# One loop for every group of four heads, a last load in halves, and six held stores in an attention-times-value kernel on Trainium2

**Chip, cores, metric.** One core of one Trainium2 chip. The metric is the device time of one execution in microseconds (us), lower is better; the profile's span is some 2 us shorter, as it runs from the first to the last instruction. Line numbers such as L124 are those of the kernel whose profile is shown; the same loop has another number in each kernel (L134 before is L124 after, L176 is L166, L161 is L151).

## The reference

```python
batch, n_heads, seq, head_dim = 8, 12, 1024, 64          # float32
attn_weights: (8, 12, 1024, 1024)      v: (8, 12, 1024, 64)
return np.einsum('bhqs,bhsd->bhqd', attn_weights, v)     # float32
```

403 MB of weights, 25 MB of v and 25 MB of output pass through the core: 96 heads, 24 groups of four.

## The kernel before

The core works in 48 units. Two units are a group of four heads: 128 partitions are 4 heads by 32, and a partition holds 32 rows of one head, 16 (the `G` row groups) in each unit. GpSimd loads a unit (8.39 MB of fp32, cast to bf16 on the way) into one of two buffers. TensorE transposes its 16 row groups, two bf16 side by side in an fp32 word, through four PSUM banks; VectorE and ScalarE copy them to SBUF; TensorE multiplies by v, the product is copied, transposed back and copied into an output slot. A group is stored as one transfer of 1 MiB. The stores of the last groups are *held*: issued only behind the last load, so that the DMA engines have work while TensorE finishes.

```python
LOOPED = NV - 1                      # 23 groups of four heads in the loop
HELD = 4
HELD_FROM = LOOPED - HELD            # groups 19 to 22 are held
BY_SYNC = HELD_FROM + 2              # 19, 20 by GpSimd; 21, 22 by SyncE
pieces_of = {                        # the last four heads: two units of two heads
    NU - 2: [(0, GH), (GH, GH)],
    NU - 1: [(0, 4), (4, 4), (8, 4), (12, 2), (14, 2)],
}
# ... cut ...
def pe_unit(i, n, loaded, it):       # TensorE, one unit
    pe.wait_ge(*loaded)
    for g in range(G):
        transpose_g(abf[i], g, n)
    wait_both(s_ot, n)
    if i == 0:
        pe.wait_ge(s_vr, it)
        spread_v(range(VH), po + px)
        wait_both(s_vbf, it * 2)
    transpose_back()                 # the unit before
    wait_both(s_last, n)
    # ... cut: 64 matmuls of 256 columns ...
with nc.Fori(1, LOOPED + 1, 1, engines=(PE,)) as it:
    # ... cut: two pe_units ...
for t in range(2):                   # the separate end: a pair of heads each, piece by piece
    # ... cut ...
# GpSimd
for n in range(NU - 2):
    pool.wait_ge(s_t[True], (n + 1) * PER_DVE)   # unit n has left its buffer
    load_attn(n + 2)
    if n % 2 == 0:
        # ... cut: load of v for the next group ...
        if 0 < q <= HELD_FROM:
            store(q - 1)
for q in range(HELD_FROM, BY_SYNC):
    store(q)
pool.drain()
# SyncE
nc.sync.wait_ge(*s_piece[NU - 1, len(pieces_of[NU - 1]) - 1])   # the last load has landed
for q in range(BY_SYNC, LOOPED):
    store(q, by_sync=True)
# ... cut: the last four heads, 0.5 + 0.25 + 0.25 MiB ...
```

## Time and profile before

| | before |
|---|---|
| time, median (range) | 1055.54 us (1055.07 to 1056.22), 4 runs; 1055.86 was the median of the first three, which the prediction knew |
| span | 1053.7 us |
| busy: TensorE, VectorE, ScalarE | 71%, 37%, 38% |
| DMA engines | full from the first to the last but one of 40 slices |
| traffic at HBM | 427.82 MB read, 25.17 MB written: 430 GB/s |

Read it from the bottom up: if the DMA engines are full, the time is the bytes over the rate, plus what isn't full at the start and the end.

### The profile page before, as it was taken

To read this page: it belongs to the slowest core of one execution; us is meant where nothing else is said; L and a number is where in the kernel's file an instruction comes from. 1 tells how busy PE (TensorE), PEld (TensorE's weight loads), DVE (VectorE), ACT (ScalarE), POOL (GpSimd) and SP (SyncE) were. 2 spreads that over 40 slices of the span, in tenths; PEclk is the share of its full clock that TensorE was granted. 3 is DMA by queue.
4 is the path that set the end of the run, shared out by engine and by line. 5 is a ranking of instruction groups with operands and counts; after the bars stand their busy time and mean duration, and the time that the engine had idled before them with its cause. 6 is when DMAs were issued, how large, how long until landed. Compare 5 with 4: busy or idle time off the path is not lost.

```text
span 1053.7 us, 16145 instructions
## 1 busy us (share of the span) xinstructions
PE 753.2 (71%) x6888; PEld 704.7 (67%) x6888; DVE 387.5 (37%) x583; ACT 404.9 (38%) x492; POOL 54.6 (5%) x106
## 2 busy tenths in 40 slices
PE   0877687866877668676786767876767767687796
PEld 0766586755867667675686666866667767677685
DVE  1543334423433234332353333433334333343353
ACT  0443334433443334433353333434334333343353
POOL 1000000000000000000000000000000000000010
PEclk9988878988888888888888878889788888898899
DMA  9999999999999999999999999999999999999998
GB/s 219 220 217 208 238 231 219 239 210 248 235 214 238 207 241 239 218 239 211 244 233 218 233 223 232 238 219 239 229 220 238 213 236 238 219 219 208 218 215 281
DMA packets 15096, 239.70 MB, mean 227 GB/s; under 512 B 1648, under 2 KB 2160, under 8 KB 5488
## 3 DMA queue, kind: packets, MB, share of 16 engines
q0 software_dynamic: 13968, 235.41, 99.6%
q1 hardware_dynamic: 1120, 4.19, 1.0%
q8 instruction: 4, 0.07, 0.0%
q14 instruction: 4, 0.03, 0.0%
HBM read 427.82 MB, written 25.17 MB: 430 GB/s over the span
## 4 chain that ended last, share of the span: by engine, by line
DMA 73%; PE 25%; issue 1%; ACT 0%; DVE 0%; POOL 0%; POOLq 0%; SPq 0%
DMA abf<-in_attn_weights_dram 73%; PE bank L134 23%; PE bank L176 1%; PE bank L161 0%; ACT at L287 0%; PE bank L149 0%; DVE at L287 0%; POOL abf L373 0%; ACT ot L306 0%; ACT osb_last L268 0%; POOLq L476 0%; SPq L83 0%
## 5 line engine op out<-in xcount | busy, mean ns | idle before, releaser
L134 PE MATMUL bank<-ident,abf 128*128 128x128 f32 x3072 | 467.6, 325 | 261.0 <-DMA abf<-in_attn_weights_dram 261.0
L134 PEld LDWEIGHTS bank<-ident,abf 128*128 128x128 f32 x3072 | 458.0, 215 | 274.1 <-DMA abf<-in_attn_weights_dram 273.3
L287 DVE COPY at<-bank 128x1024 bf16<-128x1024 bf16 x480 | 320.0, 688 | 494.0 <-PE bank L134 493.3
L287 ACT COPY at<-bank 128x1024 bf16<-128x1024 bf16 x288 | 289.0, 1012 | 425.4 <-PE bank L134 425.4
L176 PE MATMUL bank<-at,vbf 128*64 128x256 bf16 x3040 | 215.9, 279 | 1.5 <-ACT at L287 1.2
L176 PEld LDWEIGHTS bank<-at,vbf 128*64 128x64 bf16 x3040 | 195.3, 108 | 17.0 <-issue 5.2
L299 ACT COPY ot<-bank 128x512 f32<-128x512 f32 x46 | 26.9, 585 | 173.5 <-PE bank L176 173.5
L299 DVE COPY ot<-bank 128x512 f32<-128x512 f32 x46 | 31.8, 691 | 145.1 <-PE bank L176 145.1
L161 PE MATMUL bank<-ident,ot 128*128 128x128 f32 x392 | 52.4, 276 | 31.4 <-DVE vbf L261 30.9
L373 POOL DMA_DIRECT2D abf<-in_attn_weights_dram x53 | 28.2, 534 | 896.2 <-PE bank L134 895.2
L161 PEld LDWEIGHTS bank<-ident,ot 128*128 128x128 f32 x392 | 43.4, 141 | 43.9 <-DVE vbf L261 42.2
L268 ACT COPY osb<-bank 128x512 f32<-128x512 f32 x94 | 50.5, 589 | 20.8 <-PE bank L161 20.8
L261 DVE CAST vbf<-bank 128x512 bf16<-128x512 f32 x48 | 31.0, 686 | 7.3 <-PE bank L149 7.3
L261 ACT CAST vbf<-bank 128x512 bf16<-128x512 f32 x48 | 25.9, 588 | 11.8 <-PE bank L149 11.8
L149 PE MATMUL bank<-vr,spread 32*128 32x512 bf16 x384 | 26.7, 377 | 0.0
L149 PEld LDWEIGHTS bank<-vr,spread 32*128 32x128 bf16 x384 | 10.2, 92 | 7.3
L385 POOL DMA_DIRECT2D out_dram<-osb x21 | 11.3, 540 | 41.7 <-ACT osb L268 41.7
L378 POOL DMA_DIRECT2D vr<-in_v_dram x23 | 12.1, 528 | 19.2 <-PE bank L149 18.8
L287 ACT ACT_TABLE_LOAD x9 | 11.5, 1283 | 1.2 <-SPq L83 1.1
L306 ACT COPY ot<-bank 128x256 f32<-128x256 f32 (+1 forms) x3 | 1.3, 443 | 9.1 <-PE bank L176 9.1
L306 DVE COPY ot<-bank 128x256 f32<-128x256 f32 (+1 forms) x3 | 1.5, 514 | 7.4 <-PE bank L176 7.4
L360 DVE CAST vr<-v 128x2048 bf16<-128x2048 f32 x1 | 1.3, 1304 | 3.4 <-DMA v<-in_v_dram 3.4
(11 smaller groups left out, 7.1 us busy)
## 6 DMA issues: line engine op xcount, KB each, us to landing
abf<-in_attn_weights_dram POOLq DMA_DIRECT2D x46, 4096.0 KB, 33.3
out_dram<-osb POOLq DMA_DIRECT2D x21, 1024.0 KB, 34.1
vr<-in_v_dram POOLq DMA_DIRECT2D x23, 512.0 KB, 34.4
abf<-in_attn_weights_dram POOLq DMA_DIRECT2D x2, 2048.0 KB, 26.3
abf<-in_attn_weights_dram POOLq DMA_DIRECT2D x3, 1024.0 KB, 20.3
out_dram<-osb SPq DMA_DIRECT2D x2, 1024.0 KB, 8.0
v<-in_v_dram SPq DMA_DIRECT2D x1, 1024.0 KB, 5.0
abf<-in_attn_weights_dram POOLq DMA_DIRECT2D x2, 512.0 KB, 27.6
```

Of the source, the lines that this page charges most:

```text
L134: last = pe.matmul(out=pt[g % 4][:, k], lhsT=words[:, k], rhs=ident, is_transpose=True, start=(k == 0), stop=(k == KW - 1),)
L149: last = pe.matmul(out=ps, lhsT=spread[rows, b], rhs=vr[rows, b], start=(b == 0), stop=(b == VB - 1),)
L161: last = pe.matmul(out=ps[:, ds(j * P, P)], lhsT=ot[:, j0 + j], rhs=ident, is_transpose=True, start=(j == 0), stop=(j == jn - 1),)
L176: last = pe.matmul(out=outs, lhsT=vbf[:, 2 * kw + par, h], rhs=at[:, ds(half * GH + j0, jn), kw, ds(col * np_, np_), par], start=(n == 0), ...
L261: copy(out=vbf[:, :, h], in_=ps.rearrange("p (k d) -> p k d", k=SB)).then_inc(s_vbf[e])
L268: return copy(out=rows.rearrange("p (half j) d -> p j half d", half=2)[:, ds(j0, jn)], in_=ps[:, ds(0, jn * P)].rearrange("p (j half d) -> ...
L287: ins = copy(out=at[:, g].rearrange("c k j two -> c (k j two)"), in_=bank[g % 4].bitcast(bf16),)
L299: copy(out=ot.rearrange("c j (h p) -> c h j p", h=VH)[:, ds(2 * e, 2)], in_=po[e].rearrange("c (h j p) -> c h j p", h=2, j=GH),).then_inc( ...
L306: copy(out=ot.rearrange("c j (h p) -> c h j p", h=2)[:, e, ds(j0, jn)], in_=po[e].rearrange("c (j p) -> c j p", j=GH)[:, ds(j0, jn)],).the ...
L373: pool.dma_start(out=abf[n % 2][:, ds(g0, gn)].rearrange("p g s -> p (g s)"), in_=in_).then_inc(s_abf[n % 2] if k == 0 else s_piece[n, k][ ...
L378: pool.dma_start(out=vr.rearrange("p b x -> p (b x)"), in_=v_g[iv]).then_inc(s_v, 16)
L385: eng.dma_start(out=out_q[q], in_=osb[slot(q)].rearrange("p r d -> p (r d)"), **({} if by_sync else {"single_packet": True}),).then_inc(s_ ...
```

## The change

Its intent: the last four heads are treated as all others, which removes the second code path for pairs of heads. That puts more work behind the last load. Two things are to pay for it: the last two units are loaded in halves, so that only half of the last unit's transposes wait for the last bytes, and six stores are held instead of four. TensorE's loop runs the same code in every turn, so it can't wait for the halves' own semaphores in the last turn alone. SyncE therefore watches all loads in order and tells TensorE of each through one counting semaphore, `s_half`.

```diff
-    HELD = 4
-    HELD_FROM = LOOPED - HELD
-    BY_SYNC = HELD_FROM + 2
+    HELD = 6
+    HELD_FROM = NV - 1 - HELD
+    BY_SYNC = HELD_FROM + 3
 ... cut ...
-    pieces_of = {
-        NU - 2: [(0, GH), (GH, GH)],
-        NU - 1: [(0, 4), (4, 4), (8, 4), (12, 2), (14, 2)],
-    }
+    HALVED = NU - 2
 ... cut ...
             for g in range(G):
+                if g == GH:
+                    pe.wait_ge(s_half, n)
                 transpose_g(abf[i], g, n)
 ... cut ...
-        with nc.Fori(1, LOOPED + 1, 1, engines=(PE,)) as it:
+        with nc.Fori(1, NV + 1, 1, engines=(PE,)) as it:
 ... cut: TensorE's, VectorE's and ScalarE's code for the two pairs, 60 lines, removed ...
         wait_both(s_ot, NU + 1)
-        transpose_back([(0, 4, px[0])])
-        wait_both(s_last, NU)
-        multiply_pair(1, 4, 4)
-        wait_both(s_ot, NU + 2)
-        transpose_back([(4, 2, px[1]), (6, 2, bank[0])])
+        transpose_back()
 ... cut ...
+            pieces = [(0, G)] if n < HALVED else [(0, GH), (GH, GH)]
+            for g0, gn in pieces:
                 pool.dma_start(
 ... cut; the rest is SyncE's ...
+        for n in range(-2, NU - 2):
+
+            if n + 2 < HALVED:
+                nc.sync.wait_ge(s_abf[n % 2], 16 * ((n + 2) // 2 + 1))
+            else:
+                nc.sync.wait_ge(s_second[n + 2], 16)
+            nc.sync.sem_inc(s_half)
 ... cut: v and the stores' slots, as before ...
```

## The prediction

> **What bounds the kernel now.** I began with the page's slices: whichever engine is full in all forty is the bound, and the rest only has to keep it fed.
>
> ```profile
> PE   0877687866877668676786767876767767687796
> DMA  9999999999999999999999999999999999999998
> DMA packets 15096, 239.70 MB, mean 227 GB/s; under 512 B 1648, under 2 KB 2160, under 8 KB 5488
> HBM read 427.82 MB, written 25.17 MB: 430 GB/s over the span
> DMA abf<-in_attn_weights_dram 73%; PE bank L134 23%; PE bank L176 1%; PE bank L161 0%; ACT at L287 0%; PE bank L149 0%; DVE at L287 0%; POOL abf L373 0%; ACT ot L306 0%; ACT osb_last L268 0%; POOLq L476 0%; SPq L83 0%
> ```
>
> The 16 DMA engines are at nine tenths or more from the first slice to the last but one; TensorE is not. The 227 GB/s counts the bf16 that arrives; counted where it is read, as fp32, the traffic is 452.99 MB, 430 GB/s. The chain credits 23% to the transposes (L134), because a buffer is reloaded only when all 16 groups have left it. That is no loss: the other buffer's load is queued meanwhile, so DMA stays full.
>
> Next, the chain of waits in order of time, for what one store costs inside the stream:
>
> ```profile
> 828.90 9.79 PE bank L134 x64
> 872.45 10.15 PE bank L134 x64
> 916.01 10.50 PE bank L134 x64
> 957.11 10.40 PE bank L134 x64
> 998.26 10.35 PE bank L134 x64
> ```
>
> Two units (four heads) take 872.45 - 828.90 = 43.55 us, again 43.56, then 41.10 and 41.15. The short periods are those in which the kernel no longer stores: 2 x 8.389 MB of weights and 1.049 MB of v, 17.83 MB in 41.12 us, 433.5 GB/s. With a 1.049 MB store, 18.87 MB in 43.55 us, 433.4 GB/s. One stored group of four heads therefore costs 43.55 - 41.12 = 2.43 us where it lies, exactly its bytes.
>
> Last, two-microsecond windows over the end (columns: stretch, length, busy time and count of PE, PEld, DVE, ACT, POOL, then PE clock, DMA share, GB/s), and the end in order of time:
>
> ```profile
> 1036.00:1038.00 2.00, 0.84 (x7) 0.65 (x7) 0.82 (x2) 1.89 (x2) 0.00 (x0) 1.00 1.06 287
> 1042.00:1044.00 2.00, 1.65 (x16) 1.39 (x16) 1.25 (x2) 1.50 (x2) 0.00 (x0) 1.00 1.02 426
> 1048.00:1050.00 2.00, 0.00 (x0) 0.00 (x0) 0.00 (x0) 0.00 (x0) 0.00 (x0) 1.00 0.95 353
> 1050.00:1052.00 2.00, 0.00 (x0) 0.00 (x0) 0.00 (x0) 0.00 (x0) 0.00 (x0) 0.90 0.17 58
> ```
> ```profile
> 1039.59 0.82 SPq L385 DMA_DIRECT2D out_dram<-osb  x2
> 1043.76 4.40 SPq L447 DMA_DIRECT2D out_dram<-osb_last  x2
> 1046.56 0.63 PE L161 MATMUL bank<-ident,ot 128*128 128x128 f32 x4 [0.55 <-ACT ot L306]
> 1047.23 0.37 ACT L268 COPY osb_last<-bank 128x256 f32<-128x256 f32 x1 [0.81 <-PE bank L161]
> ```
>
> A store moves as many bytes as it writes, a load twice what it writes, so the GB/s column jumps from some 215 to 425 where loads give way to stores: by mixing the two rates to 287, at about 1037.4. SyncE sees the last load's semaphore at 1039.59, 2.1 us after its data. From 1037.4 the engines are full with stores alone: two held 1 MiB stores of GpSimd, two of SyncE, and the last 1 MiB in three, 5.24 MB; at 425 GB/s 12.3 us, to 1049.7. They drain at about 1050.3 and the span ends 3.4 us later. TensorE's last work is done by 1047.2, the last copy at 1047.6, and the last 0.25 MiB store is issued from 1047.6. So the two ends, drained stores and finished tail, lie within a microsecond of each other.
>
> **What the Trainium skill says.** "DMA: Bandwidth & Descriptors", section "Where 436 GB/s comes from", gives 435.2 GB/s as the fabric's ceiling. The trace agrees: 433.4 GB/s in a steady period, so no rearrangement speeds the stream; only bytes, gaps and the end are left. The same page, "Issuing engines are not separate DMA queues", says that transfers of SyncE and GpSimd share the same 16 engines and interleave; the windows agree, 426 GB/s with both storing, no more than one queue had. Its section "Anatomy of one DMA — SWDGE (gpsimd) path" puts about 2 us of fixed cost mostly on the receipt of the last write; the 2.1 us above and the 3.4 us at the end are of that kind. "TensorE: Matmul & The Clock Gate", "Part 1: The HAM clock gate", says the clock falls to half after about 3.4 us of idleness and returns after as much work. The trace agrees in kind: after 2.73 us of waiting 64 transposes took 8.02 us, after 4.53 us they took 10.35, at a granted 0.50 to 0.54 in the first 4 us.
>
> **The change part by part.** *Bytes.* The last four heads go from two pairs of heads to one group of four. Every weight, v and output byte moves once as before, at the same run lengths in DRAM (1 KB for the last stores). 0 us.
>
> *Held stores.* The loop stored groups 0 to 18; now 0 to 16. Held: 17 to 19 on GpSimd and 20 to 22 on SyncE. Two stores leave the stream of loads, which therefore ends 2 x 2.43 = 4.9 us earlier: data at 1032.5, semaphore at 1034.6. They come back after it: 7.34 MB of stores at 425 GB/s take 17.3 us, to 1049.8, against 1049.7 by the same working before. Sum: about 0. Each store was paid at 2.43 us and is now paid at 2.47.
>
> *The uniform last unit.* Before, the loads of the last unit came in five pieces, and only 2 groups (8 transposes) and half a multiply stood behind the last piece. Now eight groups and the whole multiply do. From the last semaphore, 1034.6: SyncE passes it on, about 0.1 (estimate: the gaps between engines in the chain are 0.02 to 0.28 us); 32 transposes, 4.0 us at the rate of 64 in 8.02 and 5.2 at 64 in 10.35, I take 4.7 as TensorE will have idled about 3 us; unit 46's back transposes 1.04; 64 matmuls 4.48; a gap 0.15; ScalarE's product copy 0.58; a gap 0.15; eight back transposes 1.09; VectorE's copy of the second bank 0.69. Sum 13.0 us, so the last store is issued at 1047.6. By coincidence of design that is where it is issued now, since the loads end 4.9 us earlier and the tail behind them grows from 1047.6 - 1039.6 = 8.0 us to 13.0.
>
> *SyncE's relay.* 48 semaphore increments, and one more wait in each of TensorE's units. The wait stands after eight groups, that is at least 4 us after the unit's load landed in all units but the last two; SyncE passed the same load before. SyncE's other waits in between (v, and a store's receipt, at most 2.4 us longer) lie behind transfers queued ahead of the next load, which needs some 19.4 us. So 0 us, and 0.1 once at the end, already counted.
>
> *Removed.* Four small load issues' completion costs and the pair code. TensorE's 32 matmuls of 512 columns (4.81 us) become 64 of 256 (4.48), beside DMA. 0 us.
>
> Total: 0 to +0.3 us on 1055.86. The span should end where it did, at 1053.7 to 1054, and the timed median at 1056.0.
>
> **The rivals.** *The longer tail becomes the bound.* If TensorE is cold throughout the last half (5.2) and each hand-over costs 0.2 more, the last store goes out at 1049, the engines run dry from 1049.0 or so, and 0.25 MiB with receipt lasts another 5 us: 1054.5 to 1055.5, +1 to +2 us. For it: all margins here are under a microsecond. Against: the design holds exactly two more stores, 4.9 us, for a tail 5 us longer.
>
> *Stores left for last are cheaper than inside the stream.* If the switch between reading and writing costs something, taking two stores out of the loads might save more than 2.47 each: 1055.0. Against it: 433.4 with the store and 433.5 without. If many writes in a row are slower than mixed ones, the other sign: at 353 GB/s, the rate of the window in which they run out, two stores would cost 5.9 instead of 4.9, +1 us. The full windows before speak for 410 to 426.
>
> *SyncE's relay starves a load.* If TensorE waited on it in each unit, buffers would come free later. It would take 9 us of delay per unit to empty the queue: after a load's issue (926.79) the other's data still has until 935.33 to come. I give that almost no weight. If it did happen, 1 us by 48 units would be 1100.
>
> *The clean loop is faster.* Five pieces to two, fewer instructions fetched: the windows around the pieces show no dip in DMA (0.94 to 1.08 from 1022 to 1040), so there is nothing to win; at most 0.5 us.
>
> **Range and chances.** The steady stream to about 1018 is untouched and repeats within 0.1%, as the three times of 1055.07 to 1056.22 do. What is uncertain is the end, -1.5 to +2.5 us. I put 8 in 10 on 1054.0 to 1058.5. Two per cent is 21 us, more than the whole end behind the last load, so faster or slower by that needs something that I haven't seen: 0.01 and 0.02.
>
> **What would show it.** Right: periods of 43.55 us with a store turn into 41.1 two groups earlier (from about 828.90 instead of 916.01); the GB/s column rises to 425 at about 1032.5 and stays there some 17 us; the first SyncE store is issued at about 1034.7; TensorE's transposes of the last half start there and its last copy ends at 1047 to 1048.5; no wait of TensorE on SyncE over 0.3 us. Wrong: a hole in the DMA share before the last store; 64 transposes split with a gap in the middle of each unit of the loop; periods other than 43.55; or a stores-only rate below 400 GB/s.

## The result

| | before | after |
|---|---|---|
| time, median (range) | 1055.54 us (1055.07 to 1056.22), 4 runs | 1055.54 us (1055.26 to 1055.75), 4 runs |
| span | 1053.7 us | 1053.3 us |
| last load's semaphore | 1039.6 us | 1034.3 us |
| last store issued | 1047.6 us | 1048.5 us |
| busy TensorE | 753.2 us | 754.8 us |

All outputs are right. The ratio is 0.9999, with a 95% interval of 0.9982 to 1.0017: the same. A ratio is the mean time of one kernel's fast runs over that of the other's of the same rounds, so it isn't quite the ratio of the medians.

The chain of waits of the changed kernel, in order of time (start, length, what). In its steady part the periods turn from 43.55 us (785.09 to 828.64) to 41.11 (828.64 to 869.75) where the prediction said, as the stores stop two groups earlier. Its last part is the compute tail, from SyncE's word that the last half has landed:

```profile
785.09 10.19 PE bank L124 x64
828.64 10.51 PE bank L124 x64
869.75 10.44 PE bank L124 x64
910.87 10.36 PE bank L124 x64
...
1034.29 0.02 SPq L371
1034.30 0.04 issue
1034.35 6.25 PE bank L124 x32
1040.60 0.88 PE bank L151 x8
1041.47 4.42 PE bank L166 x64
1045.89 0.02 issue
1045.92 0.59 ACT ot L256
1046.51 0.14 issue
1046.65 1.08 PE bank L151 x8
1047.73 0.02 issue
1047.75 0.69 DVE osb L227
```

The tail is 14.2 us long, to 1048.44. All its pieces are the size that was predicted (0.88 for 1.04, 4.42 for 4.48, 1.08 for 1.09) but one: the 32 transposes took 6.25 us, not 4.7.

Windows of two microseconds over the end of the changed kernel (columns as in the prediction: PE clock, DMA share and GB/s are the last three):

```profile
1032.00:1034.00 2.00, 0.00 (x0) 0.00 (x0) 0.00 (x0) 0.00 (x0) 0.00 (x0) 0.65 0.90 328
1034.00:1036.00 2.00, 1.65 (x8) 1.66 (x9) 0.49 (x1) 0.00 (x0) 0.00 (x0) 0.50 1.01 426
...
1048.00:1050.00 2.00, 0.00 (x0) 0.00 (x0) 0.44 (x1) 0.00 (x0) 0.00 (x0) 0.92 0.83 310
1050.00:1052.00 2.00, 0.00 (x0) 0.00 (x0) 0.00 (x0) 0.00 (x0) 0.00 (x0) 0.50 0.32 110
```

Loads give way to stores at about 1032.9 by the same mixing of rates as before (328 between 215 and 425); this takes the window for full, and with its share of 0.90 it comes to about 1032.5. The stores run at 426 GB/s, and TensorE starts the last half at half clock. The window from 1048 to 1050 holds the first hole behind the hand-over: a share of 0.83, where before it was 0.95. The held stores are nearly gone when the last one comes. So it meets nearly empty queues: the last two stores landed a median of 3.0 us after their issue, where before it was 5.4 (and 2.3 in the runs below in which the queues were empty). The last store goes out 0.9 us later and the span still ends 0.4 us earlier.

Who waited for whom: TensorE's waits on SyncE's relay (columns: total us, times, longest us) are one in the whole kernel, and in that one SyncE itself was waiting for the load; the relay costs 0.06 us in the chain above.

```profile
PE bank L124 <- SPq L371: 5.6, 1, 5.6
```

### The profile page after: what moved, and what is told of

Its sections match the earlier page's. It is cut to its first block, busy times and chain, and to the rows that moved or that the text cites. A ratio compares the mean times of both kernels' runs of the same rounds, so it can differ in the third digit from the quotient of the medians.

```text
span 1053.3 us, 16277 instructions
## 1 busy us (share of the span) xinstructions
PE 754.8 (72%) x6920; PEld 709.4 (67%) x6920; DVE 387.9 (37%) x582; ACT 403.3 (38%) x489; POOL 52.4 (5%) x102
## 4 chain that ended last, share of the span: by engine, by line
DMA 76%; PE 23%; issue 1%; POOL 0%; DVE 0%; ACT 0%; SPq 0%; POOLq 0%
DMA abf<-in_attn_weights_dram 76%; PE bank L124 22%; PE bank L166 0%; PE bank L151 0%; POOL abf L304 0%; DVE osb L227 0%; ACT ot L256 0%; POOLq L417 0%; SPq L371 0%; SPq L77 0%
## 5 line engine op out<-in xcount | busy, mean ns | idle before, releaser
L256 DVE COPY ot<-bank 128x512 f32<-128x512 f32 x48 | 33.2, 692 | 151.4 <-PE bank L166 151.4
L338 POOL TENSOR_SCALAR_AFFINE_SELECT spread<-spread 32x512 bf16<-32x512 bf16 x4 | 2.5, 629 | 0.6
## 6 DMA issues: line engine op xcount, KB each, us to landing
abf<-in_attn_weights_dram POOLq DMA_DIRECT2D x46, 4096.0 KB, 33.2
```

Source lines behind the costliest of these rows:

```text
L256: copy(out=ot.rearrange("c j (h p) -> c h j p", h=VH)[:, ds(2 * e, 2)], in_=po[e].rearrange("c (h j p) -> c h j p", h=2, j=GH),).then_inc( ...
L338: pool.affine_select(out=spread[ds(h * VP, VP)], in_=spread[ds(h * VP, VP)], compare_op=mybir.AluOpType.not_equal, fill=1.0, base=0, patte ...
```

## The experiments

The theory to test (A): the end is the later of two, the queue of held stores drained, and the compute tail with its last store. A held store is neutral as such. Rivals: (B) two effects that cancel, a gain from holding two more stores and a loss from the uniform end; (C) only the bytes count, and nothing at the end matters. The medians of the kernel before in the three groups of runs were 1055.35, 1055.86 and 1055.81 us; each experiment is compared with that of its own group. What follows reads differences of some 0.4% and less, so look at the ranges of the runs as well as at the intervals. `HELD` also sets, through `BY_EIGHTS`, the number of output slots and how much of ScalarE's code is looped; no effect of that shows, as the period with a store stays at some 43.55 us in every run without extra transposes.

### 1. Six held stores alone, the end in pairs kept

```diff
-    HELD = 4
-    BY_SYNC = HELD_FROM + 2
+    HELD = 6
+    BY_SYNC = HELD_FROM + 3
```

> The kernel before, its end in pairs kept, with six held stores instead of four. Theory A (the end is the later of two: the held stores drained, or the last unit's compute tail with its store; moving a store out of the load stream is neutral at 2.43 us there against 2.47 us behind it): the loads end 4.9 us earlier, the tail is done 4.9 us earlier but the stores drain at 1050 as before, so 1055.2 to 1055.8 us. Theory B (two effects that cancel: holding two more stores gains some x, the uniform end loses x; x about 1 to 5 us): faster by x, 1050.5 to 1054.5 us. Theory C (only the bytes count, whatever the end): 1055.5.

Measured: 1055.64 us (1055.38 to 1055.81), ratio 1.0002 (0.9988 to 1.0016). The last store was issued at 1042.9 instead of 1047.6, and the span stayed at 1053.8, as the queue drains when it drained before:

```profile
1048.00:1050.00 2.00, 0.00 (x0) 0.00 (x0) 0.00 (x0) 0.00 (x0) 0.00 (x0) 0.50 0.96 365
1050.00:1052.00 2.00, 0.00 (x0) 0.00 (x0) 0.00 (x0) 0.00 (x0) 0.00 (x0) 0.50 0.25 90
```

A tail that is done 4.7 us earlier won nothing. So there is no gain from held stores for B to cancel.

### 2. The uniform end alone, four held stores (run twice)

```diff
-    HELD = 6
-    BY_SYNC = HELD_FROM + 3
+    HELD = 4
+    BY_SYNC = HELD_FROM + 2
```

> The changed kernel with four held stores (two by GpSimd, two by SyncE). Theory A: the last load's semaphore comes 4.9 us later, at 1039.2; the tail behind it stays 14.2 us, so the last store is issued at 1053.3 and the span ends at 1058.2: time 1060.4 us, with a hole in the DMA share of some 4 us before the last store. Theory B: slower by its x, 1056.5 to 1060.5. Theory C: 1055.5.

Measured: 1059.81 us (1059.01 to 1060.44), ratio 1.0041 (1.0027 to 1.0055). The last load's semaphore came at 1038.9, the last store was issued at 1053.5, and ahead of it lies the hole:

```profile
1046.00:1048.00 2.00, 2.00 (x28) 1.79 (x27) 0.41 (x1) 1.24 (x3) 0.00 (x0) 1.00 0.50 209
1048.00:1050.00 2.00, 2.00 (x37) 1.95 (x36) 0.69 (x1) 0.00 (x0) 0.00 (x0) 1.00 0.66 270
1050.00:1052.00 2.00, 1.23 (x16) 0.97 (x12) 0.00 (x0) 0.59 (x1) 0.00 (x0) 1.00 0.00 0
1052.00:1054.00 2.00, 0.79 (x8) 0.55 (x6) 0.69 (x1) 0.59 (x1) 0.00 (x0) 1.00 0.03 10
```

For some 4 us the engines that bounded the kernel for a millisecond have nothing to move (0.00 and 0.03). C falls: the end matters once the tail is the later of the two. The time is 0.6 us below what was expected, as in the profiled run the span ends 4.1 us after the last store's issue when that meets empty queues (1053.5 to 1057.6), not 4.9.

The second run, made for experiment 6 on the same chip as that:

> e2_four_four once more, as the other side of e9_warm_odd on the same chip: 1059.8 us (1059.0 to 1060.4), the last 32 transposes in 6.2 to 6.8 us at a granted clock near 0.5.

Measured: 1059.93 us (1058.95 to 1060.66), ratio 1.0037 (1.0024 to 1.0051).

### 3. Seven held stores, and five

```diff
-    HELD = 6
+    HELD = 7
```

> The changed kernel with seven held stores (three by GpSimd, four by SyncE). Theory A: the loads end 2.4 us earlier (semaphore 1031.9), the last store is issued at about 1046.0 with stores still queued, the small hole of the window from 1048 to 1050 closes, and the queue drains at 1050: 1055.0 to 1055.5 us, at most 0.4 us below the changed kernel. Theory B: another x/2 faster, 0.5 to 2.5 us. Theory C: 1055.5.

Measured: 1055.61 us (1055.51 to 1056.3), ratio 1.0004 (0.9991 to 1.0018). The tail ended 3.2 us earlier (last store issued at 1045.2) and the engines drained at about 1049.9, but the span was 1053.3 as with six:

```profile
1048.00:1050.00 2.00, 0.00 (x0) 0.00 (x0) 0.00 (x0) 0.00 (x0) 0.00 (x0) 0.70 0.86 317
1050.00:1052.00 2.00, 0.00 (x0) 0.00 (x0) 0.00 (x0) 0.00 (x0) 0.00 (x0) 0.50 0.11 39
```

The hoped-for 0.4 us isn't there. B's further gain isn't either.

```diff
-    HELD = 6
-    BY_SYNC = HELD_FROM + 3
+    HELD = 5
+    BY_SYNC = HELD_FROM + 2
```

> The changed kernel with five held stores (two by GpSimd, three by SyncE). Theory A, the later of two ends: between the knee at six and the open tail at four; semaphore 1036.7, tail 14.2 to 14.6 us, last store issued at 1051.1 into empty queues, span 1055.2, time 1057.4 us. A curve without a knee (each held store worth the same) would give 1057.6 here too but would have given 1053.4 for seven, where 1055.6 was measured; so this run tests the slope of 2.4 us per store alone.

Measured: 1056.9 us (1056.27 to 1057.54), ratio 1.0013 (0.9999 to 1.0027), 0.5 us less than expected. In the profiled run, the fastest of the five (1056.27), the last 32 transposes took 5.33 us, not 6.25, and the last store went out at 1050.1. The 1.3 us between this kernel's fastest and slowest run are probably of that kind, though only one of them has a trace: with an open tail, the time depends on how long TensorE's clock stays at half, and the same 32 transposes took 5.3 to 6.7 us in the profiles of these runs. The interval touches 1; the five times lie above all of the kernel before in this group (1055.34 to 1056.1 us).

### 4. The end in pairs with two held stores

```diff
-    HELD = 4
-    BY_SYNC = HELD_FROM + 2
+    HELD = 2
+    BY_SYNC = HELD_FROM + 1
```

> The kernel before with two held stores instead of four, its end in pairs kept. Theory A: its short tail of 8.0 us was covered by four stores with little to spare; now the last load's semaphore comes at 1044.4, the last store is issued at 1052.4 into empty queues, the span ends 4.1 us later at 1056.5: time 1058.7 us. If the pieces of the pair end would hide the tail by themselves, without held stores: 1055.5.

Measured: 1058.78 us (1058.5 to 1059.06), ratio 1.0027 (1.0014 to 1.0041). The same knee in the kernel before: its pieces don't hide the tail by themselves, they make it shorter, so that four stores cover it. Put together, as a difference of means from the kernel before in the same runs:

| held stores | end in pairs (tail 8.0 us) | uniform end (tail 14.2 us) |
|---|---|---|
| 2 | +2.9 us | not run |
| 4 | 0 | +4.3, +4.2 us |
| 5 | not run | +1.2 us |
| 6 | +0.2 us | 0.0 us |
| 7 | not run | +0.4 us |

Flat on one side, sloped on the other: the shape of the later of two ends. 0.4 us and less is within the intervals; the 1.2 us at five are at the edge of theirs.

### 5. Which queue, and the halves

The last two units loaded whole, six held stores:

```diff
-    HALVED = NU - 2
+    HALVED = NU
```

> The changed kernel with the last two units loaded whole as all others, six held stores. Theory A: behind the last semaphore (still about 1034.3) stand 64 transposes, 10.4 us at the cold rate, instead of 32 in 6.25: the tail grows by 4.1 us, the last store is issued at 1052.6, the DMA engines run dry for about 3 us before it, time 1059.2 to 1059.8 us. Theory C: 1055.5. Theory B names no size for it, but says slower.

Measured: 1058.54 us (1057.41 to 1058.74), ratio 1.003 (1.0016 to 1.0043). Behind the last semaphore (1034.2) stood 64 transposes that took 9.12 us in the profiled run, the fastest of the five, and the engines ran down to a share of 0.22 between 1048 and 1052. The direction and the cause are as expected; the size is 0.7 us smaller; in the profiled run the clock recovered sooner than the 10.4 us assumed. The halves are worth some 3 us.

All six held stores by SyncE:

```diff
-    BY_SYNC = HELD_FROM + 3
+    BY_SYNC = HELD_FROM
```

> The changed kernel with all six held stores issued by SyncE after the last load's semaphore, none by GpSimd behind the loads. Theory A (stores that are already queued bridge the time between the last load's data, 1032.2, and its semaphore, 1034.3): a hole of 2.1 us plus some 1.4 us until SyncE's first data flows, then 7.34 MB at 425 GB/s, 17.3 us, to 1053: span 1056.4, time 1058.6 us. If the number of stores alone matters and not who issues them: 1055.5.

Measured: 1057.64 us (1057.25 to 1058.36), ratio 1.0016 (1.0003 to 1.003), 1.0 us less than expected. Windows over the hand-over from loads to stores:

```profile
1032.00:1034.00 2.00, 0.00 (x0) 0.00 (x0) 0.00 (x0) 0.00 (x0) 0.00 (x0) 0.53 0.16 33
1034.00:1036.00 2.00, 0.75 (x4) 0.75 (x5) 0.00 (x0) 0.00 (x0) 0.00 (x0) 0.50 0.00 0
1036.00:1038.00 2.00, 2.00 (x11) 2.00 (x10) 0.69 (x1) 0.73 (x1) 0.00 (x0) 0.50 0.96 393
```

The bulk of the last load was in at about 1032.3, SyncE learnt of it at 1035.2 and its first data flowed at 1036.0: a hole of 3.7 us in the profiled run, the slowest of the five (1058.36). In the changed kernel that stretch is filled by GpSimd's held stores, which were queued long before. So it matters who issues them: those that bridge the hand-over must be in the queue before the last load's semaphore.

All six by GpSimd:

```diff
-    BY_SYNC = HELD_FROM + 3
+    BY_SYNC = NV - 1
```

> The changed kernel with all six held stores issued by GpSimd behind the last load, SyncE storing only the last four heads. Theory A: the same bytes without a hole, drained at 1050 to 1050.5, and the same compute tail: 1055.2 to 1055.8 us. If the split between two queues is what makes the stores run at 425 GB/s, the stores-only rate falls below 400 GB/s until SyncE's first store and the time rises by 1 us or more.

Measured: 1057.97 us (1057.69 to 1058.19), ratio 1.0019 (1.0006 to 1.0033), 2 us slower than I expected. The rival that I had named for it isn't the cause: with GpSimd's stores alone the engines moved 426 GB/s. The last store was issued at 1048.9 and SyncE's last wait for it ended at 1051.7, both much as in the changed kernel (1048.5, 1051.6). The span ends 2.2 us later because of another wait: GpSimd's drain, the last instruction of its queue. One line each of that instruction for this kernel, for the changed kernel and for the one with all held stores on SyncE (the last two numbers are length in ns and start in us):

```profile
L360 POOLq DRAIN  x1: 33226/33226/33226, 1021.1 to 1021.1; - x1
```
```profile
L360 POOLq DRAIN  x1: 43769/43769/43769, 1005.4 to 1005.4; - x1
```
```profile
L360 POOLq DRAIN  x1: 34737/34737/34737, 1004.2 to 1004.2; - x1
```

It ends at 1021.1 + 33.2 = 1054.3, at 1049.2 and at 1038.9. In the first it is 4.0 us after SyncE had seen the semaphore of GpSimd's last store (1050.3), in the third 3.7 us after that of GpSimd's last load (1035.2). SyncE then waits for GpSimd, 2.2 us, which the waits of this kernel's DMA-issuing queue show and those of the changed kernel don't:

```profile
SPq L77 <- POOLq L77: 2.2, 1, 2.2
```

So, by these two runs, GpSimd's last transfer must be done some 4 us before the end, or its drain becomes a third end. Splitting the held stores three and three keeps clear of both: GpSimd's bridge the hand-over, SyncE's are last. Why the drain takes those 4 us no run shows.

### 6. The mis-sized term: the half clock

The 32 transposes of the last half were 1.55 us longer than predicted. The suspect is TensorE's clock: it had idled 5.63 us, not the 3 of the prediction. To keep it busy I put transposes of the identity, whose result nobody reads, before the wait for the second half; with four held stores, so that the tail is open and its length shows in the time.

```diff
     HELD = 4
+    DUMMY = 24
 ... cut ...
                 if g == GH:
+                    pe.wait_ge(s_cp[g - 4], n)
+                    for _ in range(DUMMY):
+                        pe.matmul(out=pt[g % 4][:, 0], lhsT=ident, rhs=ident, is_transpose=True, start=True, stop=True)
                     pe.wait_ge(s_half, n)
```

> The changed kernel with four held stores (as e2_four_four, whose compute tail lies open) and 24 transposes of the identity in each unit, whose result nobody reads, just before TensorE waits for the second half; they fill some 3.1 us of its 5.6 us of idling before the last half. If the 6.25 to 6.71 us of the last 32 transposes are the half clock after idling (theory A's account of the mis-sized term), they now take about 4.1 us at a granted clock of 1.00, the last store goes out 2.6 us earlier than in e2_four_four, and the time is about 1057.2 us against 1059.8, as long as the stream of loads isn't disturbed (period 41.1 us as before). If instead the copies of VectorE and ScalarE or the hand-over from SyncE hold these transposes, they stay at 6 us or more and the time at 1059.8.

Measured: 1058.99 us (1057.99 to 1060.68), ratio 1.0029 (1.0015 to 1.0043), an interval that overlaps that of experiment 2. The profiled run (1059.92 us, the second slowest of the five) shows the last 32 transposes in 4.04 us at a clock of 1.00, but from 1041.6, not 1039.0. The extra transposes of the units before had made TensorE late, so those of the last unit ran from 1039.02 to 1041.80, when the last half had landed at 1039.6. What the clock won was given back at once; why other runs of it were up to 1.9 us faster no trace shows. The second version has them only in the second unit of each group:

```diff
-    DUMMY = 24
+    DUMMY = 28
-                    for _ in range(DUMMY):
+                    for _ in range(DUMMY * i):
```

> As e5_warm_four (four held stores, idle transposes of the identity before the wait for the second half), but 28 of them and in the second unit of each pair of units alone, so that they don't delay the units before the last. In e5_warm_four TensorE ran 2.5 us late when the last half landed and gave back what the full clock won. Theory A: now they run in the idle time before 1037, the last 32 transposes start at about 1039.0 and take 4.1 us at clock 1.00, the last store is issued at 1051.0 instead of 1053.6, span 1055.1, time 1057.2 us, 2.6 us below e2b_four_four. If a cold clock isn't what lengthened the tail, the time stays at 1059.8.

Measured: 1057.87 us (1057.29 to 1058.09), against 1059.93 for the same kernel without them on the same chip: 2.1 us faster (the ranges don't touch). The last half's transposes in order of time, first with the extra transposes, then without:

```profile
1036.34 3.22 PE L188 MATMUL bank<-ident 128*128 128x128 f32 x28
1039.89 4.11 PE L125 MATMUL bank<-ident,abf 128*128 128x128 f32 x32 [0.33 <-SPq L375]
```
```profile
1039.95 6.63 PE L124 MATMUL bank<-ident,abf 128*128 128x128 f32 x32 [5.56 <-SPq L371]
```

Same start, same work, 2.5 us apart: the granted clock is 1.00 in the first, and 0.50 in the second until about 1045.9. The two profiled executions differ by 2.6 us in time (1058.09 and 1060.66), the medians by 2.1. The half clock is the cause. With six held stores it would probably win nothing (not run): with seven, a tail 3.2 us shorter won nothing either. None of the eleven runs has a lower median than the kernel before or the changed kernel.

## Why the prediction was right

- **The bound and the price of a store inside the stream** held: 43.55 and 41.11 us, 2.44 us for each store, two groups earlier.
- **The two ends meet** held, and experiments 1 to 4 show it as a knee rather than by two lucky numbers. The predicted drain of the held stores at 1049.8 is what the run with seven shows (about 1049.9), where no late store hides it.
- **The compute tail**: 13.0 us predicted, 14.2 measured. The mis-sized term is the 32 transposes, 6.25 us for 4.7. Two steps of its working were wrong. The prediction halved the time of 64 transposes after a wait (10.35 us, so 5.2), as if the half clock were spread evenly over them. It lies on the first of them: of those 64 the first 32 took 6.24 us (998.26 to 1004.50, mean clock 0.55) and the rest 4.11 at a clock of 1.00. So even its cold case of 5.2 was too short. And TensorE had idled 5.6 us, not about 3, which its own numbers would have given: half a unit is 4.19 MB, 9.7 us at 433.5 GB/s, less 4.1 us for the first half's transposes. The last store went out at 1048.5 instead of 1047.6. It cost nothing: it met nearly empty queues, and landed 3 us after its issue. That the room was just enough for this slip is luck; the prediction had put all margins under a microsecond.
- **Signs**: those of being right came true in the main, but not the letter of one: there is a wait of TensorE on SyncE of 5.6 us, in which SyncE itself waited for the load. One sign of being wrong, a hole in the DMA share before the last store, showed in small: the share of 0.83 from 1048 to 1050.
- **SyncE's relay** cost 0.06 us once and nothing else, as predicted.
- **The first rival**, the tail as the bound, came half true. The prediction called it +1 to +2 us at a last store issued at 1049; at 1048.5 it is level. There is no margin left in the changed kernel for the tail: with five held stores it is already 1.2 us slower.
- **The second rival**, a gain or a loss from stores left for last, did not show in experiment 1: 0.2 us, within its interval. **The third**, a starved load, did not occur; nor did a gain from fewer pieces show (the fourth).
- **Three readings** don't hold as they stand, and none bears on the total. Three load issues are removed, not four (seven pieces to four). Of the 3.4 us at the end only 1.7 lie between the drained engines and SyncE's last semaphore (1050.3 to 1052.0); the rest is the program's end. And 433.4 GB/s is counted in fp32 at HBM, while the Trainium skill's "DMA: Bandwidth & Descriptors", section "Where 436 GB/s comes from", states its ceiling of 435.2 for the ports of SBUF, where a load arrives as half as many bytes (some 215 GB/s in the windows). So the steady stream doesn't show that ceiling at work; what sets its 433 GB/s no run shows.

Where did the gain of two more held stores go? It was never a gain. Held stores are bytes moved from one full stretch to another; they are worth time only where a stretch would otherwise be empty, and the longer tail is that stretch. The change bought simpler code with 5 us of cover, and the cover cost nothing as the bytes had to be stored anyway.

## What to carry to other kernels

In a kernel whose transfers are full from end to end, ask of a change at the end only this: which of the two ends is later, the last bytes out or the last result in, and by how much. Hold back as many stores as the tail behind the last load is long (here 2.4 to 2.5 us each), queue some of them before the last load's semaphore so that they bridge the hand-over, and let the queue whose completion takes longest to report not be the last. A tail that starts after some 3 us of idleness or more has to be reckoned at TensorE's half clock for its first microseconds: in these two kernels' loops 64 transposes took 8.02 us after 2.73 us of waiting, and 9.1 to 10.6 after every wait from 2.9 us up (in the run with five held stores 9.47 after 2.54, so the limit isn't sharp).

## What the Trainium skill lacked or had wrong

- "DMA: Bandwidth & Descriptors": it says nothing of a drain of GpSimd's queue. Here the drain ended 3.7 and 4.0 us after the semaphore of GpSimd's last transfer had been seen, and cost 2.2 us of span where GpSimd stored last. None of its pages on DMA and on GpSimd has it.
- The same page, section "Measured (HBM→SBUF, 128 partitions, SWDGE, issued from GpSimd)", has 425 GB/s as its highest measured rate. The steady stream here, with the cast to bf16 and stores mixed in, moved 433.5 GB/s counted at HBM, closer to the 435.2 that the page names as the ceiling of the ports of SBUF (where these loads arrive as half as many bytes).
- "TensorE: Matmul & The Clock Gate", "Part 1: The HAM clock gate", puts the return to the full clock at around 4 us of activity, plus or minus 0.5 us. Here, after 5.5 to 5.6 us of idleness and with the same transposes, the granted clock came back about 3.0 us after their start in one run (five held stores) and about 6.1 us in another (four held, first run), by windows of two microseconds; the 32 transposes took 5.33 to 6.71 us in seven profiles, and 4.11 warm. The page also says that the window is free-running and that the count varies from run to run; the spread here is wider than its half microsecond.
